# Attention's exponentials scaled where they lie, and modulation weights loaded by blocks of rows

## The chip, the cores and the metric

The kernel runs on one core of a Trainium2 chip. The core has five engines that run side by side, each with its own stream of instructions, taken in order: TensorE (PE in the profile; its weight loads are PEld), VectorE (DVE), ScalarE (ACT), GpSimd (POOL) and SyncE (SP, which here only issues transfers). They work on an on-chip memory of 128 partitions, SBUF, and on PSUM, into which TensorE writes. Semaphores tell one engine that another has finished. The metric is the device time of one execution in microseconds; the kernel's time is the median of several.

## The reference, cut to what matters

Two layers of a diffusion transformer over 256 context and 512 latent tokens, all in fp32. From a conditioning vector each layer gets six rows of 1024 numbers, shifts, scales and gates ("modulation"). Three mixers follow one input projection, of which one is attention and one a gated delta rule; then come the output projection, a gated layer norm and an MLP.

```python
mod_l = (jax.nn.silu(c) @ mod_w[i] + mod_b[i])[:, None, :]
mod_c = (jax.nn.silu(c_ctx) @ mod_w[i] + mod_b[i])[None, None, :]

def _attend(q, k, v):
    s = jnp.einsum('bqhgd,bkhd->bhgqk', q, k).astype(jnp.float32) * (HEAD_DIM ** -0.5)
    pr = jax.nn.softmax(s, axis=-1).astype(v.dtype)
    return jnp.einsum('bhgqk,bkhd->bqhgd', pr, v)
```

Attention has six query heads on two key heads of 64. A latent query sees all 768 keys, a context query the 256 context keys. The second layer needs only latent queries.

## The kernel before

**The order of the work.** The kernel is written as Python generators (scans, preparations, attention, modulation, projections), each of which issues a few instructions and yields. A planner, the class `Flow` (lines 40 to 195), keeps a planned time for each engine and tile from `cost` (line 74) and steps the generator whose planned time is lowest; tasks of the delta rule carry a bias that puts them ahead. So the order of instructions on each engine is set at build time by those estimates, and is then fixed. Every operation passes through one recorder, so all traced instructions have one line, L207; tiles tell them apart. PSUM is lent out in two kinds, four `mm` tiles of 128x512 and two `ax` tiles of 128x1024.

**The stage that the change touches.** Tokens come in tiles of 128: two of context, four latent. In each layer attention (`attention`, line 1041, and `att_out`, line 1095) runs side by side with the delta rule (`dn_make`, `dn_scan`, `dn_gate`, lines 1492 to 1595): roughly 320 to 590 us in layer 0, with all six tiles, and 1475 to 1690 us in layer 1, with the four latent ones. The scan is a chain of small matmuls (`S,rW`, `rr,rT`, `vn,rK`, `S,rQ`, `vn,rA` in the order's rows), and SP loads its `rT` tiles from scratch in HBM.

**Attention.** For each head: scores into an `ax` tile (`akh,qs` and `akl,qs`), the negated maximum `anm` on VectorE, the exponential `ape` on ScalarE with its sum, transposes of `ape` through an `mm` tile (`c_ident,ape`), copies into `apT` or `akT` on ScalarE, and for two heads together the product with the values (`apT,ava`, `akT,ava`). `ape` has two buffers. After six heads the reciprocals `ars` of the six sums are spread over partitions by twelve matmuls (`c_ident,ars`; six in the program), copied to `abc`, and multiplied into the output `ayb`, which is stored.

**Modulation.** `mod` (line 389) makes rows of the modulation: `cz` (the two conditioning vectors, 32 columns a block) times weights `modw`, K of 1024 in eight blocks of 128 rows, and n pieces of 512 columns that go to n groups of 32 partitions of one PSUM tile. Then the bias is added into `modb` and the rows are transposed (`c_ident,modb`). During layer 0's stage above, `mods` (line 859) runs `mod` for j=1 (n=4) and j=2 (n=2): 48 loads of 256 KB through four buffers. Stage 0 makes j=0 with `mod_in` (line 452), and later rows are made on VectorE in the MLP; the change touches neither.

**Layer 1's end.** `rest` (line 1645) starts the output projection. Its weights `wraw` (16 loads of 512 KB over both layers, rounded to `whi` by ScalarE) lie in memory that the delta rule's pool has used, so SP waits for the last gated output `zg`; broadcasts `lg`, `lb` and `g` stand in the same queue.

Of the kernel before, what the change touches and what calls it, by code (L numbers as in the profile page):

```python
# [8 lines left out]
F32 = mybir.dt.float32  # L9
F32R = mybir.dt.float32r  # L10
AF = mybir.ActivationFunctionType
ALU = mybir.AluOpType
# [4 lines left out]
P = 128  # L17
# [22 lines left out]
class Flow:  # L40
# [33 lines left out]
    def cost(self, eng, op, out, ins, kw):  # L74
        n = max([self.width(out)] + [self.width(a) for a in ins])
        if eng == "tensor":
            n, m = self.width(out), out.shape[0]
            if op == "transpose":
                return 0.87 * n
            if ins[-1].dtype == F32R:  # L80
                return max(35.0 + 0.56 * m, 0.42 * n)

            return (1.0 if m == 64 else 2.0) * max(35.0 + 0.62 * m, 0.83 * n)
        if eng == "vector":
            fast = op in ("tensor_copy", "tensor_scalar") and ins[0].tensor.name not in self.lent
            return 66.0 + n * (0.53 if fast else 1.04) + (60.0 if op == "scalar_tensor_tensor" else 0.0)
        if eng == "scalar":
            return 100.0 + 0.8 * n
        if eng == "gpsimd":
            return 160.0 + n * (170.0 if kw.get("op") == ALU.pow else 1.0 if op == "memset" else 2.1)  # L90
        return 4.0 * n * out.shape[0] / 340.0
# [133 lines left out]
def _half(f):  # L225
    return slice(64 * f, 64 * f + 64)


class Feed:
# [15 lines left out]
    def load(self):  # L245
        i = len(self.raws)
        src, n = self.srcs[i]
        t = self.pool.tile([P, WCOL], F32, tag="wraw", bufs=self.raw, name="wraw")[:, 0:n]
        self.k.nc.sync.dma_start(out=t, in_=src)
        self.raws.append(t)  # L250
# [34 lines left out]
class K:  # L285
# [103 lines left out]
    def mod(self, l, j, n, wt, bt, bufs):  # L389


        nc, d, flow = self.nc, self.d, self.flow
        mb = bt()
        nc.gpsimd.memset(mb, 0.0)
        for g in range(n):
            nc.sync.dma_start(
                out=mb[32 * g : 32 * g + 2, :], in_=d["mod_b"][l, j, g * 512 : g * 512 + 512].partition_broadcast(2)
            )
        ws = []

        def load(i):
            w = wt()
            nc.sync.dma_start(out=w, in_=d["mod_w"][l, j, i // n][:, (i % n) * 512 : (i % n) * 512 + 512])
            ws.append(w)

        for i in range(bufs):
            load(i)
        yield
        pm = yield from self.psum(512)
        for i in range(n * KD):  # L410
            k, g, w = i // n, i % n, ws.pop(0)
            yield flow.ready[w.tensor.name][0]
            nc.tensor.matmul(pm[32 * g : 32 * g + 32], self.cz[:, k, :], w, start=(k == 0), stop=(k == KD - 1))
            if i + bufs < n * KD:
                load(i + bufs)
                if i + bufs == n * KD - 1:
                    flow.signal(f"mw{l}{j}")
            yield
        ms = mb
        nc.vector.tensor_tensor(out=ms[0 : 32 * n], in0=pm[0 : 32 * n], in1=mb[0 : 32 * n], op=ALU.add)  # L420
        self.drop(pm)
        yield
        pt = yield from self.psum(512)
        for c in range(4):
            self.tr(pt[:, c * P : c * P + P], ms[:, c * P : c * P + P])
        yield
        ptv = pt.rearrange("p (c g s) -> p g c s", c=4, g=4)
        mt = self.modT[l]

        def take(name, g0, add):  # L430
            o = mt[name].rearrange("p (g c) s -> p g c s", g=2)
            nc.vector.tensor_scalar(out=o, in0=ptv[:, g0 : g0 + 2, :, 0:2], scalar1=float(add), scalar2=None, op0=ALU.add)

        def gate(w, g0):
            for s in range(2):
                for g in range(2):
                    r = 32 * (g0 + g) + s
                    nc.sync.dma_start(out=self.gates_d[l, w, s, g * 512 : g * 512 + 512].unsqueeze(0), in_=ms[r : r + 1, :])

        if j == 0:  # L440
            take("sh1", 0, 0)
            take("sc1", 2, 1)
        elif j == 1:
            gate(0, 0)
            take("sh2", 2, 0)
        else:
            take("sc2", 0, 1)
        self.drop(pt)
        self.flow.signal(f"mod{l}{j}")
        yield  # L450
# [223 lines left out]
class Kernel(K):  # L674
# [23 lines left out]
    def mix(self, l, xp, xh, xl, rest):  # L698
# [158 lines left out]
        AT.append(self.a_tiles(l, self.dn, 2))  # L857

        def mods():
            wt = lambda: self.dn.tile([P, 512], F32, tag="modw", bufs=4, name="modw")  # L860
            bt = lambda: self.dn.tile([P, 512], F32, tag="modb", bufs=1, name="modb")
            yield from self.mod(0, 1, 4, wt, bt, 4)
            yield from self.mod(0, 2, 2, wt, bt, 4)

        def makes(p):
            yield f"prep{l}{p}"
# [174 lines left out]
    def attention(self, l, at):  # L1041


        nc, ap_ = self.nc, self.a2
        qT, kT, va = at["qT"], at["kT"], at["va"]
        kh = ap_.tile([P, 2, TOK], F32R, name="akh")
        kl = ap_.tile([P, 2, TOK], F32R, name="akl")
        for c in (slice(0, CTX), slice(CTX, TOK)):
            for j in range(2):
                src = kT[_half(j), c]  # L1050
                for a in range(2):
                    nc.scalar.activation(out=kh[_half(a), j, c], in_=src, func=AF.Copy)
                for a in range(2):
                    nc.vector.tensor_tensor(out=kl[_half(a), j, c], in0=src, in1=kh[_half(j), j, c].bitcast(F32), op=ALU.subtract)
                yield
        late = None
        for t in self.tiles:
            n = CTX if t < 2 else TOK
            sl = slice(t * P, t * P + P)

            qs = ap_.tile([P, 3, 2, P], F32R, tag="qs", bufs=1, name="qs")
            for h2 in range(2):
                a, b = _half(h2), _half(1 - h2)
                nc.scalar.activation(out=qs[a, :, h2, :], in_=qT[a, :, sl], func=AF.Copy, scale=0.125)
                nc.vector.scalar_tensor_tensor(
                    out=qs[b, :, h2, :], in0=qT[a, :, sl], scalar=0.125, in1=qs[a, :, h2, :].bitcast(F32), op0=ALU.mult, op1=ALU.subtract
                )
            yield

            st = {"su": self.small([P, NH], "asu"), "pT": (ap_.tile([P, TOK], F32, tag="apT", bufs=1, name="apT"), kT)}  # L1070
            for m, h in enumerate(HEADS):
                q = qs[:, h // 2, h % 2, :]
                px = yield from self.psum(1024)
                ps = px[:, 0:n]
                for c in range(0, n, 512):
                    e = min(n, c + 512)
                    nc.tensor.matmul(ps[:, c:e], q, kh[:, h // 3, c:e], start=True, stop=False)
                    nc.tensor.matmul(ps[:, c:e], q, kl[:, h // 3, c:e], start=False, stop=True)
                yield
                if late:  # L1080
                    yield late
                nm = self.small([P, 1], "anm")
                nc.vector.tensor_reduce(out=nm, in_=ps, axis=AX.X, op=ALU.max, negate=True)
                yield
                i = NH * t + m
                if i - NH * self.tiles[0] > 1:
                    yield f"po{l}{i - 2}"
                pe = ap_.tile([P, TOK], F32, tag="ape", bufs=2, name="ape")
                nc.scalar.activation(out=pe[:, 0:n], in_=ps, func=AF.Exp, bias=nm[:, 0:1], accum_out=st["su"][:, h : h + 1])
                self.drop(ps)  # L1090
                yield
                late = self.att_out(l, t, m, n // P, pe, va, st)
        yield late

    def att_out(self, l, t, m, kts, pe, va, st):
# [29 lines left out]
        yield  # L1125
        if m < NH - 1:
            return

        rs = self.small([P, NH], "ars")
        nc.vector.reciprocal(rs, st["su"])  # L1130
        yield
        pb = yield from self.psum(384)
        for h in range(NH):
            nc.tensor.matmul(
                pb[_half(h % 2), h // 2 * P : h // 2 * P + P], rs[:, h : h + 1].broadcast_to([P, HD]), self.ident, start=True, stop=True
            )
        yield
        bc = ap_.tile([P, 384], F32, tag="abc", bufs=1, name="abc")
        nc.scalar.copy(bc, pb)
        self.drop(pb)  # L1140
        yield
        y = ap_.tile([P, 3, P], F32, tag="ayb", bufs=1, name="ayb")
        nc.vector.tensor_tensor(out=y, in0=pv, in1=bc.rearrange("p (a q) -> p a q", a=3), op=ALU.mult)
        self.drop(st["po"])
        yield from self.store(self.y_d[l, t, :, 2:5, :], y)

# [810 lines left out]
```

## Time and profile before

| | |
|---|---|
| median of 3 runs | 2119.76 us (2119.71 to 2125.24) |
| the profiled execution | 2125.93 us, span 2123.9 us |
| mean granted TensorE clock | 0.941 |
| TensorE busy | 1952.7 us, 92% |
| VectorE busy | 1339.7 us, 63% |
| ScalarE busy | 922.1 us, 43% |
| moved by DMA | 208.92 MB, mean 98 GB/s |

The span is the profiled execution from its first to its last instruction; the rest of its 2125.93 us lies around it. Busy shares are means over stages with different limits, so a term of a sum is read in the window where it lies. "Idle before, releaser" says what ended the wait of an engine. PEclk is the clock granted to TensorE as a share of 2.4 GHz; its other level, 1.2 GHz, shows as 0.50.

### The profile page before, as it was taken

Reading aid. Unit: us, or ns where it says so; the run is one execution under the profiler, and the core shown is the slowest. Engines: PE = TensorE matmul, PEld = TensorE weight load, DVE = VectorE, ACT = ScalarE, POOL = GpSimd, SP = SyncE. Lnnn points to the kernel's source line nnn. Section 1 sums busy time; section 2 is a strip of 40 time slices with the busy share of each in tenths; the row PEclk is TensorE's granted clock in tenths of the full one; section 3 lists DMA queues with packets and bytes.
Section 4 is the critical chain, followed back from the end, with each engine's and each line's share of the span. In section 5 each row is a group of like instructions: output and inputs, shape, how many; then the busy total and the mean of one; then the engine's idle time right before and its main releaser. Section 6 shows DMA issues by size and latency. Waiting matters only on the chain.

```text
span 2123.9 us, 31022 instructions
## 1 busy us (share of the span) xinstructions
PE 1952.7 (92%) x11960; PEld 1592.9 (75%) x11960; DVE 1339.7 (63%) x2499; ACT 922.1 (43%) x1881; POOL 195.3 (9%) x375
## 2 busy tenths in 40 slices
PE   6999779999998999999999989987898888999998
PEld 2788554667777888888888778776777668888886
DVE  5578787675477436362457776889785475544455
ACT  4444336467645422322232274543766535432331
POOL 1111211000012000000000111122100010000001
PEclk8999989989999999999999979977898999999999
DMA  7311014312335325241345233101101335332231
GB/s 278 101 45 51 26 49 142 106 56 58 126 107 185 119 74 166 80 139 45 135 160 184 88 136 96 52 34 33 28 20 28 119 127 186 119 100 80 85 114 60
DMA packets 98241, 208.92 MB, mean 98 GB/s; under 512 B 30851, under 2 KB 45059, under 8 KB 98093
## 3 DMA queue, kind: packets, MB, share of 16 engines
q1 hardware_dynamic: 86956, 189.24, 27.3%
q10 hardware_dynamic: 11136, 17.70, 2.3%
q8 instruction: 94, 1.54, 0.3%
q14 instruction: 55, 0.44, 0.1%
HBM read 184.38 MB, written 17.79 MB: 95 GB/s over the span
## 4 chain that ended last, share of the span: by engine, by line
PE 65%; DVE 16%; ACT 6%; issue 5%; POOL 4%; DMA 4%; SPq 0%; ACTq 0%; POOLq 0%; DVEq 0%
PE mm L207 41%; PE ax L207 24%; DVE cacc L207 2%; DVE wlo L207 2%; DVE tm L207 2%; DVE Xx L207 1%; POOL crn L207 1%; DVE M L207 1%; DVE A L207 1%; DMA wraw<-in_w_out 1%; POOL rs L207 1%; DVE axn L207 1%; DMA wraw<-in_w_up 1%; DVE st L207 1%; DMA modw<-in_mod_w 1%
## 5 line engine op out<-in xcount | busy, mean ns | idle before, releaser
L207 ACT ACTIVATE whi<-wraw 128x1024 fp32r<-128x1024 f32 (+2 forms) x188 | 195.1, 1050 | 449.7 <-PE ax L207 287.7
L207 DVE TENSOR_TENSOR wlo<-wraw,whi 128x1024 fp32r<-128x1024 f32 (+2 forms) x188 | 226.7, 1212 | 233.1 <-ACT whi L207 232.4
L207 PE MATMUL mm<-x2xh,whi 128*128 128x256 f32 (+1 forms) x832 | 287.0, 345 | 10.5 <-ACT whi L207 9.1
L207 PE MATMUL mm<-x2xl,whi 128*128 128x256 f32 (+1 forms) x832 | 286.3, 344 | 0.0
L207 PE MATMUL mm<-x2xh,wlo 128*128 128x256 f32 (+1 forms) x832 | 284.6, 342 | 0.9 <-DVE wlo L207 0.9
L207 PE MATMUL ax<-whi,hh 128*128 128x512 f32 x640 | 251.1, 392 | 0.1
L207 PE MATMUL ax<-wlo,hh 128*128 128x512 f32 x640 | 250.0, 391 | 0.1
L207 PE MATMUL ax<-whi,hl 128*128 128x512 f32 x640 | 249.9, 391 | 0.0
L207 PEld LDWEIGHTS mm<-x2xh,whi 128*128 128x128 f32 x832 | 159.2, 191 | 33.2 <-ACT whi L207 10.0
L207 DVE TENSOR_TENSOR acc<-acc,ax 128x1024 f32<-128x1024 f32 x68 | 82.9, 1219 | 148.2 <-PE ax L207 148.1
L207 PEld LDWEIGHTS mm<-x2xh,wlo 128*128 128x128 f32 x832 | 158.6, 191 | 20.2 <-DVE wlo L207 1.4
L207 PEld LDWEIGHTS mm<-x2xl,whi 128*128 128x128 f32 x832 | 159.0, 191 | 17.5
L207 PEld LDWEIGHTS ax<-whi,hh 128*128 128x128 f32 x640 | 120.2, 188 | 29.8 <-ACT hh L207 5.6
L207 PEld LDWEIGHTS ax<-wlo,hh 128*128 128x128 f32 x640 | 120.2, 188 | 27.4 <-issue 2.6
L207 PEld LDWEIGHTS ax<-whi,hl 128*128 128x128 f32 x640 | 120.1, 188 | 27.3 <-DVE hl L207 2.9
L207 DVE SCALAR_TENSOR_TENSOR acc<-modw,cz,acc 128x1024 f32<-128x1024 f32 x80 | 101.2, 1280 | 8.6 <-DMA acc<-in_mod_b 5.4
L207 ACT ACTIVATE rl<-mm 128x256 f32<-128x256 f32 (+1 forms) x104 | 50.5, 489 | 127.3 <-PE mm L207 127.3
L207 POOL TENSOR_SCALAR rs<-mv 128x1 f32<-128x1 f32 x52 | 33.0, 635 | 684.2 <-DVE mv L207 681.9
L207 PE MATMUL mm<-whi,yh 128*128 128x512 f32 x160 | 64.8, 415 | 10.7 <-ACT whi L207 9.3
L207 DVE TENSOR_REDUCE anm<-ax 128x1 f32<-128x768 f32 (+1 forms) x60 | 50.7, 847 | 36.2 <-PE ax L207 35.9
L207 DVE TENSOR_TENSOR hl<-rl,hh 128x768 fp32r<-128x768 f32 (+2 forms) x76 | 54.4, 716 | 28.0 <-ACT hh L207 28.0
L207 ACT ACTIVATE v<-mm,sh,sc 128x128 f32<-128x128 f32 x152 | 58.2, 463 | 29.3 <-PE mm L207 24.5
(256 smaller groups left out, 4276.7 us busy)
## 6 DMA issues: line engine op xcount, KB each, us to landing
wraw<-in_w_up SPq DMA_DIRECT2D x64, 512.0 KB
wraw<-in_w_down SPq DMA_DIRECT2D x64, 512.0 KB
modw<-in_mod_w SPq DMA_DIRECT2D x56, 512.0 KB
modw<-in_mod_w SPq DMA_DIRECT2D x80, 256.0 KB
wraw<-in_w_ch SPq DMA_DIRECT2D x22, 512.0 KB
wraw<-in_w_out SPq DMA_DIRECT2D x16, 512.0 KB
x_d<-xt ACTq DMA_DIRECT2D x16, 512.0 KB
xt<-x_d SPq DMA_DIRECT2D x14, 512.0 KB
```

The costliest lines, as they stand in the source:

```text
L207: return f(*args, **kw)
```

## The change

Three edits. First, `cost` prices a matmul of 32 rows by 512 columns at 0.6 ns a column, 307 ns, where it was 850; this shifts the planned times, and with them the order. Second, `mod` loads the n pieces of a block of rows in one transfer (1 MB for j=1, 512 KB for j=2; 16 loads for 48) and runs its n matmuls one after the other; in `mods` there is one buffer of 128x2048 in place of four of 128x512. Third, attention takes the reciprocal of each head's sum on VectorE and multiplies the exponentials by it in place, before they are transposed; the twelve matmuls, `abc` and the product go, and ScalarE copies the output from PSUM.

```diff
@@ cost
+            if m == 32 and n == 512:
+                return 0.6 * n
             return (1.0 if m == 64 else 2.0) * max(35.0 + 0.62 * m, 0.83 * n)
@@ mod
-        def load(i):
-            w = wt()
-            nc.sync.dma_start(out=w, in_=d["mod_w"][l, j, i // n][:, (i % n) * 512 : (i % n) * 512 + 512])
+        def load(k):
+            w = wt()[:, 0 : 512 * n]
+            nc.sync.dma_start(out=w, in_=d["mod_w"][l, j, k][:, 0 : 512 * n])
             ws.append(w)
...
-        for i in range(n * KD):
-            k, g, w = i // n, i % n, ws.pop(0)
+        for k in range(KD):
+            w = ws.pop(0)
             yield flow.ready[w.tensor.name][0]
-            nc.tensor.matmul(pm[32 * g : 32 * g + 32], self.cz[:, k, :], w, start=(k == 0), stop=(k == KD - 1))
-            if i + bufs < n * KD:
-                load(i + bufs)
-                if i + bufs == n * KD - 1:
-                    flow.signal(f"mw{l}{j}")
+            for g in range(n):
+                nc.tensor.matmul(
+                    pm[32 * g : 32 * g + 32], self.cz[:, k, :], w[:, 512 * g : 512 * g + 512], start=(k == 0), stop=(k == KD - 1)
+                )
+            if k + bufs < KD:
+                load(k + bufs)
             yield
@@ mods
-            wt = lambda: self.dn.tile([P, 512], F32, tag="modw", bufs=4, name="modw")
+            wt = lambda: self.dn.tile([P, 2048], F32, tag="modw", bufs=1, name="modw")
...
-            yield from self.mod(0, 1, 4, wt, bt, 4)
-            yield from self.mod(0, 2, 2, wt, bt, 4)
+            yield from self.mod(0, 1, 4, wt, bt, 1)
+            yield from self.mod(0, 2, 2, wt, bt, 1)
@@ attention
-                nc.scalar.activation(out=pe[:, 0:n], in_=ps, func=AF.Exp, bias=nm[:, 0:1], accum_out=st["su"][:, h : h + 1])
+                su = self.small([P, 1], "asu")
+                nc.scalar.activation(out=pe[:, 0:n], in_=ps, func=AF.Exp, bias=nm[:, 0:1], accum_out=su)
                 self.drop(ps)
                 yield
+                rs = self.small([P, 1], "ars")
+                nc.vector.reciprocal(rs, su)
+                nc.vector.tensor_scalar(out=pe[:, 0:n], in0=pe[:, 0:n], scalar1=rs[:, 0:1], scalar2=None, op0=ALU.mult)
+                yield
@@ att_out
-        rs = self.small([P, NH], "ars")
-        nc.vector.reciprocal(rs, st["su"])
...
-        bc = ap_.tile([P, 384], F32, tag="abc", bufs=1, name="abc")
-        nc.scalar.copy(bc, pb)
...
         y = ap_.tile([P, 3, P], F32, tag="ayb", bufs=1, name="ayb")
-        nc.vector.tensor_tensor(out=y, in0=pv, in1=bc.rearrange("p (a q) -> p a q", a=3), op=ALU.mult)
+        nc.scalar.copy(y, pv)
```

Since the planner sets the order, the change moves instructions. The rows that follow are of TensorE's order in layer 0's stage, in the second half of the modulation rows j=1; `modw,cz` are the modulation matmuls, the others steps of scans. First of before:

```order
1190 L207 MATMUL mm_67<-rr,rT_2721 128x128 x2
1191 L207 MATMUL mm_67<-vn,rK_2726 128x128 x2
1192 L207 MATMUL mm_69<-modw,cz 32x512
1193 L207 MATMUL mm_68<-S,rW_2742 128x128 x2
1194 L207 MATMUL mm_69<-modw,cz 32x512
1195 L207 MATMUL mm_68<-rr,rT_2747 128x128 x2
1196 L207 MATMUL mm_69<-modw,cz 32x512
1197 L207 MATMUL mm_68<-vn,rK_2752 128x128 x2
1198 L207 MATMUL mm_69<-modw,cz 32x512
1199 L207 MATMUL mm_68<-S,rQ_2757 128x128 x2
1200 L207 MATMUL mm_68<-vn,rA_2762 128x128 x2
```

The same place of the changed kernel (`kq` are key-query products of a later scan step, `c_ident,modb` the transposes that end j=1):

```order
1170 L210 MATMUL mm_66<-S,rQ_2757 128x128 x2
1171 L210 MATMUL ax_71<-akh,qs 128x256
1172 L210 MATMUL ax_71<-akl,qs 128x256
1173 L210 MATMUL mm_69<-modw,cz 32x512 x4
1174 L210 MATMUL ax_70<-kq 64x128 x8
1175 L210 MATMUL mm_69<-modw,cz 32x512 x20
1176 L210 MATMUL mm_69<-c_ident,modb 128x128 x4
1177 L210 MATMUL mm_69<-S,rW_2742 128x128 x2
1178 L210 MATMUL mm_69<-rr,rT_2747 128x128 x2
1179 L210 MATMUL mm_69<-vn,rK_2752 128x128 x2
```

Where single modulation matmuls stood between the steps of scans, 20 of them, the last five blocks of rows, now stand in one piece, ahead of the transposes and the next step `S,rW`.

SP's order at the same place, with the loads of `modw` and of `rT`. First of before:

```order
53 L207 DMA rT_2695<-TT_1019 64x2x64 x2
54 L207 DMA modw<-in_mod_w 128x512 x2
55 L207 DMA rT_2695<-TT_1019 64x2x64 x2
56 L207 DMA modw<-in_mod_w 128x512 x6
57 L207 DMA rT_2773<-TT_1024 64x2x64
58 L207 DMA modw<-in_mod_w 128x512
59 L207 DMA rT_2773<-TT_1024 64x2x64 x3
60 L207 DMA modw<-in_mod_w 128x512
```

and of the changed kernel:

```order
50 L210 DMA rT_2695<-TT_1019 64x2x64 x4
51 L210 DMA rT_2773<-TT_1024 64x2x64 x2
52 L210 DMA modw<-in_mod_w 128x2048
53 L210 DMA rT_2773<-TT_1024 64x2x64 x2
54 L210 DMA modw<-in_mod_w 128x2048 x3
55 L210 DMA modw<-in_mod_w 128x1024
56 L210 DMA gates_d<-modb 1x512 x4
57 L210 DMA rT_2747<-TT_1019 64x2x64 x2
58 L210 DMA rT_2721<-TT_1024 64x2x64
```

The last three loads of j=1 and the first of j=2 follow each other on SP; the loads of `rT` and the rows' stores to `gates_d` come behind them.

The last place is TensorE's order at the end of layer 1's stage; `whi,yh` is the first matmul of the output projection, `zg` the gated output of the delta rule. First of before:

```order
6479 L207 MATMUL mm_69<-akT,ava 64x128
6480 L207 MATMUL mm_69<-apT,ava 64x128
6481 L207 MATMUL mm_69<-akT,ava 64x128
6482 L207 MATMUL mm_69<-apT,ava 64x128
6483 L207 MATMUL mm_69<-akT,ava 64x128
6484 L207 MATMUL ax_70<-c_ident,zg 128x128 x4
6485 L207 MATMUL mm_67<-whi,yh 128x512
```

and of the changed kernel:

```order
6405 L210 MATMUL ax_71<-akh,qs 128x512
6406 L210 MATMUL ax_71<-akl,qs 128x512
6407 L210 MATMUL ax_71<-akh,qs 128x256
6408 L210 MATMUL ax_70<-c_ident,zg 128x128 x4
6409 L210 MATMUL ax_71<-akl,qs 128x256
6410 L210 MATMUL mm_69<-c_ident,ape 128x128 x4
6411 L210 MATMUL mm_66<-c_ident,ape 128x128 x2
6412 L210 MATMUL ax_70<-akh,qs 128x512
6413 L210 MATMUL ax_70<-akl,qs 128x512
6414 L210 MATMUL ax_70<-akh,qs 128x256
```

The transposes of `zg` stood behind attention's last product and just ahead of the projection; now they stand among the scores of the last heads. On SP the broadcasts `lg`, `lb` and `g`, which followed the first three loads of the projection's weights, now precede them.

## Rows read from the trace of the kernel before

**Rows 1.** The page: busy times (1) and the chain that ended last (4).

```profile
PE 1952.7 (92%) x11960; PEld 1592.9 (75%) x11960; DVE 1339.7 (63%) x2499; ACT 922.1 (43%) x1881; POOL 195.3 (9%) x375
...
PE 65%; DVE 16%; ACT 6%; issue 5%; POOL 4%; DMA 4%; SPq 0%; ACTq 0%; POOLq 0%; DVEq 0%
```

**Rows 2.** Windows: start:end, length, busy us (instructions) by engine, PEclk, DMA, GB/s.

```profile
320.00:590.00 270.00, 246.19 (x1960) 179.45 (x1958) 167.38 (x498) 167.20 (x512) 17.10 (x46) 0.94 0.31 95
...
1475.00:1690.00 215.00, 183.95 (x1715) 153.60 (x1716) 146.64 (x450) 142.07 (x417) 22.54 (x93) 0.88 0.14 37
...
1400.00:1500.00 100.00, 78.11 (x727) 64.53 (x726) 86.19 (x209) 50.63 (x107) 26.18 (x97) 0.76 0.12 37
...
1500.00:1600.00 100.00, 89.81 (x744) 75.40 (x746) 83.48 (x270) 65.00 (x196) 2.04 (x3) 0.97 0.09 20
```

**Rows 3.** Tile modw, 250 to 480 us: the matmuls, and TensorE's waits.

```profile
L207 PE MATMUL mm<-modw,cz x96: 592/617/1063, 318.9 to 433.3; 128*32 128x512 f32 x96
...
  DMA modw<-in_mod_w: 1.8, 4
```

**Rows 4.** Timeline, TensorE: start us, us, operation, xcount; then [idle before].

```profile
34.85 2.77 PE L207 MATMUL mm<-modw,cz 128*32 128x512 f32 x12
...
363.00 1.05 PE L207 MATMUL mm<-modw,cz 128*32 128x512 f32 x4
...
363.98 0.71 PE L207 MATMUL mm<-S,rQ 128*128 128x128 f32 x4
...
366.91 1.05 PE L207 MATMUL mm<-modw,cz 128*32 128x512 f32 x2
...
367.89 0.44 PE L207 MATMUL mm<-c_ident,gs 128*128 128x128 f32 x2
```

**Rows 5.** Timeline, SP's issue and ScalarE's start: two 512 KB loads landing.

```profile
1684.60 1.29 SPq L207 DMA_DIRECT2D wraw<-in_w_out  x3
...
1688.38 1.06 ACT L207 ACTIVATE whi<-wraw 128x1024 fp32r<-128x1024 f32 x1 [3.19 <-DMA wraw<-in_w_out]
...
1689.76 1.06 ACT L207 ACTIVATE whi<-wraw 128x1024 fp32r<-128x1024 f32 x1 [0.32 <-DMA wraw<-in_w_out]
```

**Rows 6.** Windows (columns as in rows 2) around that place.

```profile
1685.00:1690.00 5.00, 0.51 (x1) 0.50 (x2) 0.53 (x1) 1.49 (x3) 0.00 (x0) 0.50 0.89 288
...
1690.00:1695.00 5.00, 4.96 (x16) 3.47 (x15) 3.15 (x3) 1.87 (x2) 0.00 (x0) 0.72 1.03 391
```

**Rows 7.** Waits of TensorE, 320 to 590 us: total us, times, longest.

```profile
PE ax L207 <- DVE zg L207: 3.1, 2, 2.7
...
PE mm L207 <- ACT whi L207: 2.6, 1, 2.6
```

**Rows 8.** Groups by form: operation xcount | busy us, mean ns | idle before.

```profile
L207 PE MATMUL mm<-c_ident,ars 128*64 128x128 f32 x120 | 10.9, 280 | 0.0
...
L207 DVE RECIPROCAL ars<-asu 128x6 f32<-128x6 f32 x10 | 1.9, 190 | 3.1 <-ACT ape L207 3.0
...
L207 DVE TENSOR_TENSOR ayb<-mm,abc 128x384 f32<-128x384 f32 x10 | 5.5, 551 | 4.9 <-ACT abc L207 4.9
...
L207 ACT COPY abc<-mm 128x384 f32<-128x384 f32 x10 | 4.8, 483 | 8.3 <-PE mm L207 8.2
...
L207 DVE TENSOR_SCALAR be<-be 128x72 f32<-128x72 f32 x2 | 0.4, 204 | 0.0
...
L207 DVE TENSOR_TENSOR M<-M,be 128x768 f32<-128x768 f32 x12 | 11.0, 948 | 0.0
...
L207 DVE TENSOR_REDUCE anm<-ax 128x1 f32<-128x768 f32 x48 | 45.7, 954 | 30.3 <-PE ax L207 30.1
```

**Rows 9.** Timeline of TensorE at layer 1's end; waits of SP, 1600 to 1700.

```profile
1683.41 1.12 PE L207 MATMUL ax<-c_ident,zg 128*128 128x128 f32 x4 [3.03 <-DVE zg L207]
...
1689.49 0.79 PE L207 MATMUL mm<-whi,yh 128*128 128x512 f32 x1 [4.97 <-ACT whi L207]
...
SPq L207 <- DVE zg L207: 20.5, 1, 20.5
```

More of the change, by code (lines that the diff above doesn't have):

```diff
@@ L399, in mod @@
         ws = []
-        def load(i):
-            w = wt()
-            nc.sync.dma_start(out=w, in_=d["mod_w"][l, j, i // n][:, (i % n) * 512 : (i % n) * 512 + 512])
+        def load(k):
+            w = wt()[:, 0 : 512 * n]
+            nc.sync.dma_start(out=w, in_=d["mod_w"][l, j, k][:, 0 : 512 * n])
             ws.append(w)
-        for i in range(bufs):
-            load(i)
+        for k in range(bufs):
+            load(k)
         yield
         pm = yield from self.psum(512)
-        for i in range(n * KD):
-            k, g, w = i // n, i % n, ws.pop(0)
+        for k in range(KD):
+            w = ws.pop(0)
             yield flow.ready[w.tensor.name][0]
-            nc.tensor.matmul(pm[32 * g : 32 * g + 32], self.cz[:, k, :], w, start=(k == 0), stop=(k == KD - 1))
-            if i + bufs < n * KD:
-                load(i + bufs)
-                if i + bufs == n * KD - 1:
-                    flow.signal(f"mw{l}{j}")
+            for g in range(n):
[4 more added lines that the diff above has]
+                load(k + bufs)
             yield
@@ L1068, in attention @@
             yield
-            st = {"su": self.small([P, NH], "asu"), "pT": (ap_.tile([P, TOK], F32, tag="apT", bufs=1, name="apT"), kT)}
+            st = {"pT": (ap_.tile([P, TOK], F32, tag="apT", bufs=1, name="apT"), kT)}
             for m, h in enumerate(HEADS):
@@ L1127, in att_out @@
             return
-        rs = self.small([P, NH], "ars")
-        nc.vector.reciprocal(rs, st["su"])
[L1131 to L1137, printed above, removed]
-        bc = ap_.tile([P, 384], F32, tag="abc", bufs=1, name="abc")
-        nc.scalar.copy(bc, pb)
-        self.drop(pb)
-        yield
         y = ap_.tile([P, 3, P], F32, tag="ayb", bufs=1, name="ayb")
-        nc.vector.tensor_tensor(out=y, in0=pv, in1=bc.rearrange("p (a q) -> p a q", a=3), op=ALU.mult)
+        nc.scalar.copy(y, pv)
         self.drop(st["po"])
```

## The prediction, made before the changed kernel ran

> **What bounds the kernel now.** I read the page first. TensorE is busy for 92% of the span, VectorE for 63% and ScalarE for 43%, and the chain that ended last runs through TensorE for 65% [rows 1]. So work taken off TensorE is worth its own length, and a stretch in which TensorE can do nothing is lost, unless it shortens a later wait. Then I cut out the two stretches in which attention and the delta rule run, by windows: in layer 0 (320 to 590 us) TensorE works 246.2 of 270 us and VectorE 167.4; in layer 1 (1475 to 1690 us) 184.0 of 215 and 146.6 [rows 2]. In layer 0, then, TensorE idles for 24 us in all, and VectorE has some 100 us free; in layer 1, 31 and 68. Third, the tile view of the modulation weights: their 48 loads cost TensorE 1.8 us of waiting in four waits, so four small buffers hide the transfers almost wholly [rows 3]. That is the cover that the change takes away.
>
> **Modulation weights: TensorE's work.** A modulation matmul (two instructions) holds TensorE for 0.98 us: 366.91 to 367.89. Two of them on different groups of 32 columns take the same 0.98 us: 363.00 to 363.98 [rows 4]. The timeline has for the 32 matmuls of the first block of rows (j=1) 17 lone ones, five pairs, a slow first three (3.5 us) and two in a row on one column group (1.9): 22 x 0.98 + 5.4 = 27 us. For the 16 of j=2 it has seven pairs and two lone ones, 8.8 us. After the change a load feeds four (j=1) or two (j=2) matmuls that stand next to each other. Six matmuls in pairs took 2.77 us, 0.92 a pair [rows 4]; that four on four column groups also take one 0.98 is not in the trace. So j=1 takes between 8 x 0.98 = 8 us (four together) and 8 x 2 x 0.92 = 15 us (two pairs); j=2 takes 8. The gain is 13 to 20 us. I take 13, from the pairs, which the trace shows.
>
> **Modulation weights: the waits.** There is one buffer. Load k+1 may start only when the last matmul of block k has read it, and the next matmul waits for the landing. What that costs depends on what stands between two blocks in TensorE's order. TensorE's order (the first piece shown with the change) has it: after the third block eight small matmuls, and then 20 modulation matmuls without anything between, that is five blocks of 1 MB, one behind the other. TensorE takes its instructions in order, so nothing covers those loads. The price of one: 512 KB issued at 1684.60 let ScalarE begin at 1688.38, 3.8 us later, and the second 512 KB of the same burst 1.4 us after that [rows 5]; so 1 MB takes about 5.2 us. No load of 1 MB stands in this kernel, so I bound it by 3.8 (that 1 MB lands as 512 KB do) and 6.0 (2.4 us of start, and 1 MB at the 288 GB/s of that window [rows 6]). Five loads: 5 x 5.2 = 26, less 1 for the eight small matmuls: +25 (18 to 29). Between the first three blocks stand 17 to 19 rows of other work each: +2 (0 to 5). The eight loads of j=2 are 512 KB, 3.8 us each, with two to six short matmuls between them and the last two side by side; I put 0 to 2 us on six of them and 3.7 on the last: +7 (3 to 12). What waits behind this: on TensorE the transposes of the modulation rows and the next scan step; on SP the loads of rT, which follow the blocked weight loads in its order; on VectorE the sum of bias and matmul. None of it can come sooner, and all then comes together.
>
> A long idle also lowers the clock that TensorE is granted. Between 1685 and 1690 us it worked 0.51 us and the clock stood at 0.50, that is 1.2 GHz; in the next 5 us, busy throughout, the mean was still 0.72 [rows 6], so some 2.8 us of them ran at the lower level and gave up 1.4. One such recovery is 1.4; the serial blocks, whose matmuls run in between, and the stretch behind may see more. I take +3 (0 to 6). Against it, ScalarE and VectorE catch up while TensorE stands, so later waits shrink. The largest waits in the stretch add up to 3.1 and 2.6 us, both not near this place [rows 7]: I take -2 (-4 to 0).
>
> The Trainium skill speaks on both sides here. "DMA: Bandwidth & Descriptors", section Bandwidth, asks for batches of at least 1 MiB and gives 6.15 us for 1 MB; by that figure the five loads would be 31 us and the sum 5 higher (an estimate from that page). "Trainium Kernel Development and Optimization", Best Practices, asks for double buffers, so that DMA and compute overlap; the change keeps the first rule and breaks the second. The trace bears out the second: four buffers leave 1.8 us of waiting [rows 3].
>
> **Attention: what goes.** For each of ten tiles 12 instructions with the reciprocal sums, 10.9 us in all [rows 8]: six tiles in layer 0, -5 after their overlap with neighbours (-6.5 to -4); four in layer 1, of which the last stand in a stretch that waits anyway, -2. On VectorE one reciprocal (0.19) and one product (0.55) go per tile; on ScalarE a copy of 0.48 is replaced by another of the same size. The last tile of layer 0 loses a link between its matmuls and the store: -1.
>
> **Attention: what comes.** For each of 60 heads a reciprocal 128x1 (as 0.19) and a scaling of the exponentials in place stand between exponential and transposes. No tensor-by-scalar operation of this size is in the trace. The nearest by operation takes 0.20 us at 128x72, the nearest by size is a tensor-by-tensor product 128x768, 0.95 us [rows 8]. I take 0.95, for size decides. Layer 0 then gets 24 x 1.14 + 12 x 0.6 - 6 x 0.74 = 30 us more on VectorE, layer 1 24 x 1.14 - 4 x 0.74 = 24 us. Both fit in the free 100 and 68 us of [rows 2], so I charge only the delay: a head's chain (maximum 0.95, exponential, transposes) gets 1.2 to 1.3 us longer. Two score tiles and two exponential tiles are in flight, so most of that hides behind the other head's matmuls and the scans. Bounds: nothing, or 6 (layer 0) and 8 (layer 1), from some six heads each in which nothing else is left. I take +2 and +3. The Trainium skill ("VectorE: DVE Perf Modes", the perf-mode tier table) gives fp32 tensor-by-scalar work in SBUF twice the rate of tensor-by-tensor: 0.5 us as an estimate, by which the +3 would be +2 and the rival on VectorE less likely; no row here shows it.
>
> **The end of layer 1.** Now TensorE waits 3.03 us for the gated delta output (zg) and then 4.97 us for the first rounded tile of the output weights [rows 9], because those weights are loaded into memory that is free only when zg is done; SP waits 20.5 us for it [rows 9]. In the new order the transposes of zg stand two heads of attention earlier, so the loads and three 512 KB broadcasts run behind the attention. The 8 us can't all go, since attention's last chain then ends the stage: -6 (-9 to 0).
>
> **The sum.** Layer 0: 25 + 2 + 7 + 3 - 2 - 13 - 5 - 1 + 2 = +18. Layer 1: -6 - 2 + 3 = -5. Together +13. The profiled execution took 2125.93 us (span 2123.9), so 2139 in its frame; it lies 6 us above the median of 2119.76. Against the median: 2133 us, slower by 0.6%.
>
> **The rivals.**
> Faster: the wider loads pay. Each of the five waits costs 3.8 instead of 5.2, four matmuls run as one (-20 instead of -13), j=2 costs 3, the clock does not fall and layer 1 gives 9. 18 + 2 + 3 - 2 - 20 - 5 - 1 + 2 - 9 - 2 + 3 = -11, 2109 us. It decides at an exposed wait of about 3 us per block if the rest stays as in my sum. For it: 390 GB/s stands in a window of this trace [rows 6], which is 2.7 us for 1 MB. Against it: the first landing alone takes 3.8. It is also what the page's rule on batches would promise. Chance 0.22.
> No change: the five waits are there, but the other engines use them to run ahead. TensorE idles 24 us in layer 0's stretch; if 10 to 12 of them come back instead of 2, the sum is +3 to +5, 2124 us. Against it: waits in this stretch are many and short. Chance 0.15.
> Slower still: VectorE becomes the bound where scan and scaling meet. In layer 1 VectorE works 86.2 of 100 us from 1400 to 1500 and 83.5 from 1500 to 1600 [rows 2], so of the 24 us some 15 have no gap, and layer 0's last heads lose 6: 13 + 15 + 4 = +32, 2152 us. It decides once the scaling takes near 0.95 us and the heads fall in the full slices. Chance 0.13.
> My forecast, 2126 to 2150: chance 0.50.
>
> **How the numbers follow.** The range 2106 to 2156 holds the forecast and nearly all of the others; below lies part of the first rival, above the upper bounds of the loads with the third. A difference under 0.3% (6 us) can't be told from none. Faster: the first rival, 0.22. Same: the second and the near edge of the forecast, 0.17. Slower: the rest, 0.61.
>
> **What would show it.** In the changed kernel's tile view of the modulation weights, TensorE's waits for their DMA should be 30 to 40 us in some 13 waits, five of them near 5 us in a row, with VectorE idle there and the granted clock below 1. The modulation matmuls should hold TensorE 16 to 23 us instead of 36. The reciprocal matmuls are gone; the scaling should take 0.5 to 0.95 us. At the end of layer 1 the wait for the output weights should be under 2 us. If the five waits are below 3 us each, or work stands between them, the forecast is wrong on the low side; if VectorE is above 95% in layer 1's stretch, on the high side.

## The result and the profile after

The changed kernel takes 2152.64 us in the median (2151.01 to 2157.53), the kernel before, run beside it, 2121.44: ratio 1.0148, 95% interval 1.0125 to 1.0171. It is slower by 31 us, where I had forecast 13. The two profiled executions, 2125.93 and 2151.97 us, differ by 26.

The page of the changed kernel, busy times and the chain that ended last; [rows 1] are the same of before:

```profile
PE 1930.1 (90%) x11840; PEld 1582.0 (74%) x11840; DVE 1366.9 (64%) x2599; ACT 924.4 (43%) x1881; POOL 195.2 (9%) x375
...
PE 61%; DVE 18%; issue 7%; ACT 6%; DMA 4%; POOL 3%; SPq 0%; ACTq 0%; DVEq 0%; POOLq 0%
```

TensorE is busy 23 us less than before, VectorE 27 us more, and the span is 26 us longer: it is waiting that grew. To see where, I cut both traces at the same instructions: layer 0's stage from the first transpose `c_ident,gs` to the first matmul of the projection `whi,yh`, and layer 1's in the same way. Windows of the changed kernel (columns as in rows 2), layer 0 and layer 1:

```profile
319.90:625.40 305.50, 233.95 (x1887) 175.47 (x1887) 183.04 (x560) 168.46 (x515) 19.13 (x58) 0.86 0.28 86
...
1521.50:1723.20 201.70, 173.99 (x1574) 143.91 (x1570) 155.13 (x479) 141.89 (x413) 20.25 (x79) 0.92 0.19 52
```

and of the kernel before:

```profile
318.00:587.40 269.40, 245.37 (x1959) 178.44 (x1959) 166.71 (x500) 167.33 (x515) 18.88 (x57) 0.94 0.31 98
...
1477.90:1689.50 211.60, 180.74 (x1623) 150.47 (x1619) 143.30 (x440) 140.17 (x412) 20.05 (x79) 0.89 0.14 36
```

Layer 0's stage grew by 36.1 us, while TensorE's work in it fell by 11.4; its idle time went from 24.0 to 71.6 us. Layer 1's stage lost 9.9 us, and the projection behind it (first to last `whi,yh`) went from 58.2 to 50.0, another 8.2. What is left to the 26 us is 1.9 before layer 0's stage and 6.2 in the rest.

Where did layer 0 lose it? TensorE's timeline of the changed kernel at the modulation matmuls of j=1 (x8 is four matmuls; the idle time before and its cause stand in brackets; [rows 4] are single ones and pairs):

```profile
345.40 1.06 PE L210 MATMUL mm<-modw,cz 128*32 128x512 f32 x8
...
351.64 1.94 PE L210 MATMUL mm<-modw,cz 128*32 128x512 f32 x8 [4.57 <-DMA modw<-in_mod_w]
...
358.96 1.94 PE L210 MATMUL mm<-modw,cz 128*32 128x512 f32 x8 [5.38 <-DMA modw<-in_mod_w]
...
366.00 1.93 PE L210 MATMUL mm<-modw,cz 128*32 128x512 f32 x8 [5.11 <-DMA modw<-in_mod_w]
...
372.80 1.93 PE L210 MATMUL mm<-modw,cz 128*32 128x512 f32 x8 [4.87 <-DMA modw<-in_mod_w]
...
379.59 1.94 PE L210 MATMUL mm<-modw,cz 128*32 128x512 f32 x8 [4.86 <-DMA modw<-in_mod_w]
```

Five blocks, one behind the other, each after a wait of 4.6 to 5.4 us: 24.8 us. The full list of TensorE's waits in the stage begins with them (total, times, longest; [rows 7] are two of before):

```profile
PE mm L210 <- DMA modw<-in_mod_w: 32.2, 10, 5.4
...
PE mm L210 <- DVE gs L210: 6.4, 4, 4.6
...
PE mm L210 <- DVE ape L210: 4.4, 3, 2.2
...
PE ax L210 <- ACT ape L210: 4.2, 5, 1.8
...
PE mm L210 <- ACT apT L210: 3.4, 5, 1.1
```

And the windows of that place in the changed kernel, 10 us each:

```profile
350.00:360.00 10.00, 2.98 (x16) 0.40 (x16) 5.75 (x12) 2.22 (x2) 0.00 (x0) 0.53 0.56 169
...
360.00:370.00 10.00, 2.83 (x16) 0.20 (x8) 0.00 (x0) 0.00 (x0) 0.00 (x0) 0.50 0.42 123
...
370.00:380.00 10.00, 2.34 (x12) 0.40 (x16) 0.00 (x0) 0.00 (x0) 0.00 (x0) 0.50 0.52 192
...
380.00:390.00 10.00, 8.13 (x33) 5.53 (x26) 2.77 (x9) 0.56 (x2) 1.57 (x3) 0.50 0.20 60
```

and of the kernel before, for the 40 us together:

```profile
350.00:390.00 40.00, 37.11 (x217) 20.45 (x208) 23.27 (x76) 17.55 (x59) 0.00 (x0) 1.00 0.45 136
```

From 360 to 380 us VectorE and ScalarE did nothing at all, and TensorE's granted clock stood at 0.50 to 0.53, that is at or near 1.2 GHz, through the serial blocks and until 390. Before, TensorE was busy for 37.1 of these 40 us at the full clock; now it is busy for 16.3. The same four matmuls take 1.06 us at 345.40 and 1.93 us here.

### The profile page after: what moved, and what is told of

Read it like the earlier page. It is cut to its first block, busy times and chain, and to the rows that moved or that the text cites. A ratio compares the mean times of both kernels' runs of the same rounds, so it can differ in the third digit from the quotient of the medians.

```text
span 2150.0 us, 30808 instructions
## 1 busy us (share of the span) xinstructions
PE 1930.1 (90%) x11840; PEld 1582.0 (74%) x11840; DVE 1366.9 (64%) x2599; ACT 924.4 (43%) x1881; POOL 195.2 (9%) x375
## 4 chain that ended last, share of the span: by engine, by line
PE 61%; DVE 18%; issue 7%; ACT 6%; DMA 4%; POOL 3%; SPq 0%; ACTq 0%; DVEq 0%; POOLq 0%
PE mm L210 38%; PE ax L210 23%; DVE cacc L210 2%; DVE wlo L210 2%; DVE tm L210 2%; DVE Xx L210 2%; DMA modw<-in_mod_w 2%; POOL crn L210 1%; DVE M L210 1%; DMA wraw<-in_w_up 1%; DVE A L210 1%; DMA wraw<-in_w_out 1%; POOL rs L210 1%; DVE axn L210 1%; DVE st L210 1%
## 5 line engine op out<-in xcount | busy, mean ns | idle before, releaser
L210 PEld LDWEIGHTS ax<-whi,hl 128*128 128x128 f32 x640 | 120.1, 188 | 27.4 <-DVE hl L210 2.9
L210 PE MATMUL mm<-modw,cz 128*32 128x512 f32 x160 | 47.1, 772 | 39.7 <-DMA modw<-in_mod_w 39.7
L210 DVE SCALAR_TENSOR_TENSOR cacc<-cb,cw,cacc 128x772 f32<-128x772 f32 (+1 forms) x72 | 70.0, 973 | 0.7 <-ACT cacc L210 0.2
```

The source lines that it names most:

```text
L210: return f(*args, **kw)
```

## The experiments

All lengths are cut as above. "Wait" is TensorE's wait for `modw` in layer 0's stage, "busy" TensorE's busy time there, "projection" the one behind layer 1's stage; ratios are against runs of the kernel before on the same chip. These runs had a median of 2122.97 us beside e1_att to e4_plan, 2116.22 beside e4b_ready to e5_small and 2121.24 beside the last two, so kernels of different groups are compared by ratio and not by median.

| kernel | median us | ratio (95%) | wait | layer 0 | busy | layer 1 | projection |
|---|---|---|---|---|---|---|---|
| before | 2121.44 | | 0.3 | 269.4 | 245.4 | 211.6 | 58.2 |
| changed | 2152.64 | 1.0148 (1.0125 to 1.0171) | 32.2 | 305.5 | 234.0 | 201.7 | 50.0 |
| e1_att | 2110.15 | 0.995 (0.9931 to 0.9968) | 0.4 | 268.7 | 239.6 | 202.4 | 50.4 |
| e2_mod | 2157.26 | 1.0176 (1.0152 to 1.02) | 27.4 | 305.6 | 243.0 | 207.1 | 56.3 |
| e3_two | 2115.23 | 0.9968 (0.9952 to 0.9985) | 3.9 | 267.3 | 232.5 | 203.3 | 50.4 |
| e4_plan | 2163.79 | 1.0197 (1.0152 to 1.0241) | 1.7 | 267.5 | 228.8 | 202.5 | 50.4 |
| e4b_ready | 2102.91 | 0.9931 (0.9906 to 0.9956) | 0.7 | 256.1 | 225.6 | 202.5 | 52.0 |
| e7_cost | 2139.55 | 1.0096 (1.0059 to 1.0133) | 25.4 | 299.5 | 233.6 | 201.8 | 52.3 |
| e8_light | 2115.63 | 0.999 (0.997 to 1.0009) | 1.6 | 262.4 | 228.3 | 211.6 | 58.7 |
| e5_small | 2104.82 | 0.9941 (0.992 to 0.9963) | 1.7 | 267.9 | 237.9 | 198.6 | 50.1 |
| e9_ars | 2113.79 | 0.9971 (0.9951 to 0.9991) | 1.1 | 275.1 | 248.6 | 204.2 | 52.5 |
| e4b_again | 2103.65 | 0.9932 (0.9907 to 0.9957) | 0.9 | 255.6 | 225.0 | 202.2 | 52.1 |

My theory was that the exposed loads make the loss and attention's part the gain in layer 1. The rival was that the scaling on VectorE costs layer 0 half of its loss. The first two kernels split the change.

**Attention's part alone.** The diff is that of `attention` and `att_out` shown with the change; `cost`, `mod` and `mods` are those of before.

> Attention's part alone on the kernel before (modulation and its price in the plan as before). Theory A, that the loss is the exposed loads of the modulation weights and that attention's part gains in layer 1: TensorE waits under 4 us for modw, layer 0's stage (first c_ident,gs to first whi,yh) within 8 us of the 269 us of before, layer 1's stage and projection some 18 us shorter, 2103 to 2114 us. Rival B, that the reciprocals and scalings on VectorE cost layer 0 some 15 us or more: layer 0's stage 284 us or longer, 2120 us or more.

The window of layer 0's stage:

```profile
314.90:583.60 268.70, 239.61 (x1886) 170.31 (x1886) 184.19 (x559) 167.93 (x515) 19.68 (x58) 0.96 0.33 98
```

It is faster than the kernel before by 0.5%. VectorE has 17 us more work in layer 0's stage than before (184.2 for 166.7), and the stage is 0.7 us shorter. Rival B falls. Layer 1's stage and projection are 17.0 us shorter together, where 18 were expected.

**Modulation's part alone.** The diffs of `cost`, `mod` and `mods`; attention of before.

> Modulation's part alone (one load a block, one buffer, the new price in the plan), attention as before. Theory A: TensorE waits 28 to 36 us for modw, layer 0's stage 28 to 40 us longer than before, layer 1 as before: 2145 to 2165 us. Rival B: the waits are there but layer 0's stage is only 10 to 20 us longer, 2130 to 2142 us.

Its wait, among TensorE's waits in layer 0's stage:

```profile
PE mm L210 <- DMA modw<-in_mod_w: 27.4, 7, 5.2
```

The whole loss of layer 0 is here: its stage is as long as the changed kernel's (305.6 for 305.5), though the waits are a little under the 28 to 36 us expected. "Layer 1 as before" was a miss. The window of layer 1's stage:

```profile
1516.80:1723.90 207.10, 175.71 (x1622) 146.17 (x1618) 143.92 (x441) 140.09 (x412) 20.66 (x83) 0.91 0.15 38
```

Stage and projection are 6.4 us shorter than before, although attention is that of before and both waits of [rows 9] are still there (3.03 and 5.12 us). In the stage TensorE idles as long as before (31.4 for 30.9 us) and is busy 5.0 us less, at a mean clock of 0.91 for 0.89. So not all of what layer 1 gains belongs to attention.

**Two buffers of half the size.** A block of j=1 comes as two loads of 512 KB, and the second is under way while the first is used.

```diff
-            wt = lambda: self.dn.tile([P, 2048], F32, tag="modw", bufs=1, name="modw")
+            wt = lambda: self.dn.tile([P, 1024], F32, tag="modw", bufs=2, name="modw")
...
-            nc.sync.dma_start(out=w, in_=d["mod_w"][l, j, k][:, 0 : 512 * n])
+            nc.sync.dma_start(out=w, in_=d["mod_w"][l, j, k][:, 1024 * h : 1024 * h + 1024])
```

> The changed kernel with two buffers of 128x1024 in place of one of 128x2048, the same memory: loads of 512 KB, two matmuls each, the next load under way while a block is used. Theory A: waits for modw fall from 32 to under 8 us, layer 0's stage 270 to 282 us, 2105 to 2120 us. Rival B: the stage stays at 290 us or more, since attention holds it; 2128 us or more.

The wait falls from 32.2 to 3.9 us and the stage from 305.5 to 267.3, a little under the range of theory A, in the same memory.

**The same buffer, another order.** Is it the 1 MB load behind one buffer that costs, or that nothing stands between the blocks? The planner's `note` gives a load a start by SP's planned time and its source; it doesn't know that the tile has to be read out first. So in the plan all loads come early, and the blocks may follow each other. This kernel moves SP's planned time to the end of the last planned matmul ahead of each later load, in `mod` and also in `mod_dve`, which makes later modulation rows on VectorE and loads their weights on the same queue:

```diff
@@ mod
             if k + bufs < KD:
+                flow.free["sync"] = max(flow.free.get("sync", 0.0), flow.free["tensor"])
                 load(k + bufs)
...
@@ mod_dve
             if k + bufs < KD:
+                flow.free["sync"] = max(flow.free.get("sync", 0.0), flow.free["tensor"])
                 load(k + bufs)
```

> The changed kernel, one buffer of 128x2048 as it is, but the plan is told that a load starts only after the matmuls that free the buffer; the order then puts scans and scores between the blocks. Theory A (what costs is the order, the blocks without work between them, not the load of 1 MB): waits for modw under 10 us, none over 3, layer 0's stage 268 to 280 us, 2100 to 2118 us. Rival C (a 1 MB load behind one buffer costs by itself, in any order): waits for modw of 20 us or more, 2130 us or more.

TensorE's waits, the first line in layer 0's stage, the others from 660 to 1480 us:

```profile
PE mm L210 <- DMA modw<-in_mod_w: 1.7, 1, 1.7
...
PE mm L210 <- DVE acc L210: 18.7, 2, 14.8
...
PE mm L210 <- ACT xn L210: 13.4, 4, 5.1
...
PE ax L210 <- DVE y L210: 11.4, 1, 11.4
```

In the stage it does what theory A said: one buffer, loads of 1 MB, a wait of 1.7 us in all, 267.5 us. The order made the loss. Yet the kernel is the slowest of all, and the time stands elsewhere: from the end of layer 0's projection to layer 1's stage it takes 864.6 us, where before took 814.5. The last three lines are waits there, 43.5 us together (`acc` is the sum that `mod_dve` makes). The edit pushes SP's planned time for all that comes later, and ahead of each load of `mod_dve` once more: 20 of these loads were issued only between 1188.7 and 1229.2 us, where before had 4 left after 1150. Which of the two places cost it is not separated. So I told the plan of the landing alone, and in `mod` alone:

```diff
             nc.sync.dma_start(out=w, in_=d["mod_w"][l, j, k][:, 0 : 512 * n])
+            if k >= bufs:
+                t, e = flow.ready[w.tensor.name]
+                flow.ready[w.tensor.name] = (max(t, flow.free["tensor"] + 2200.0 + 4.0 * 512 * n * P / 340.0), e)
```

> The changed kernel, one buffer, with only the landing of each later block told to the plan (not earlier than the matmuls before it plus the load), and nothing else of the plan's clock for SP moved, as e4_plan did. Theory A: waits for modw under 8 us, layer 0's stage 264 to 274 us, and the 48 us that e4_plan lost between the stages gone: 2100 to 2118 us. Rival: the loss between the stages belongs to the order of the blocks; it stays, 2145 us or more.

Two blocks of j=1 in TensorE's timeline:

```profile
366.07 1.07 PE L210 MATMUL mm<-modw,cz 128*32 128x512 f32 x8
...
373.53 1.07 PE L210 MATMUL mm<-modw,cz 128*32 128x512 f32 x8
```

and the windows of the stage and of the 40 us in which the changed kernel stood:

```profile
317.70:573.80 256.10, 225.61 (x1887) 170.07 (x1887) 182.83 (x560) 167.11 (x515) 19.03 (x57) 0.94 0.34 103
...
350.00:390.00 40.00, 37.15 (x283) 27.03 (x283) 26.85 (x100) 22.78 (x81) 0.00 (x0) 1.00 0.46 138
```

No block of j=1 has a wait ahead of it, and TensorE is busy for 37 of the 40 us at the full clock. The stage is 8 us shorter than theory A's range, and the loss between the stages is gone (816.3 us). This kernel beats both: 0.9931 (0.9906 to 0.9956). It was run a second time:

> The kernel of e4b_ready once more, with more rounds and on the chip of e9_ars, for the interval: ratio to before 0.990 to 0.996, layer 0's stage 254 to 260 us, waits for modw under 2 us.

0.9932, and the stage at 255.6 us, confirm it.

**The price in the plan.** The changed kernel with the old price, 850 ns a modulation matmul.

> The changed kernel with the old price of a modulation matmul in the plan (850 ns for 307). Theory A (one buffer that the plan doesn't see makes the bare blocks): 16 matmuls still stand in one piece, waits for modw 24 to 36 us, 2140 to 2165 us. Rival D (the lower price packs the blocks together): waits under 12 us, 2125 us or less.

The wait is 25.4 us and the kernel 0.96% slower than before, so the new price isn't the cause, though some of the loss is its: 16 matmuls in one piece instead of 20, and three waits of 4.7 to 5.6 us in a row for five.

**Less TensorE work in layer 0's stage of the kernel before.** The theory had a hole: the modulation matmuls' saving didn't show. In e3_two and e4_plan TensorE is 13 to 17 us less busy than before, and the stage is only 2 us shorter. This kernel leaves out most columns of 42 of the 48 matmuls:

```diff
-            nc.tensor.matmul(pm[32 * g : 32 * g + 32], self.cz[:, k, :], w, start=(k == 0), stop=(k == KD - 1))
+            c = 512 if k == 0 else 64
+            nc.tensor.eng.matmul(pm[32 * g : 32 * g + 32, 0:c], self.cz[:, k, :], w[:, 0:c], start=(k == 0), stop=(k == KD - 1))
```

> The kernel before; of the 48 modulation matmuls of layer 0's stage the 42 after the first block of rows work on 64 columns in place of 512 (the rest of the sum is left out), loads and planned prices as before. It takes some 25 us of work off TensorE in that stage. Theory E (the work saved there is given back as waits, since scans and attention's tail set the stage): the stage gets 0 to 10 us shorter, 2112 to 2121 us. Rival F (TensorE bounds the stage, as predicted): 18 us or more shorter, 2103 us or less.

The window of layer 0's stage:

```profile
318.00:580.40 262.40, 228.29 (x1958) 183.16 (x1958) 166.33 (x500) 166.96 (x515) 19.04 (x57) 0.92 0.33 100
```

TensorE is 17.1 us less busy, not 25: the modulation matmuls hold it for 16.4 us instead of 38.0 (an instruction of 64 columns still takes 0.24 us, and a matmul is two), and the rest of its busy time is 4.5 us more, at a mean clock of 0.92 for 0.94. The stage is 7.0 us shorter, and the kernel's time the same within its interval. Six tenths of the work taken off came back as waits. That speaks for theory E, not for all of it.

**Less VectorE work in attention.** e1_att with the scaling on 32 columns only.

> Attention's part alone (as e1_att), with the scaling on 32 of the 768 or 256 columns (the others stay unscaled), planned price as before: VectorE loses some 20 us of work and each head's chain 0.4 us. Theory G (attention's chain sets the tail after the last scan): that tail falls from 61 to 55 us or less, 2098 to 2106 us against 2110 of e1_att. Rival H (the chain is hidden): within 3 us of e1_att.

From the last scan step's first matmul (`S,rW`) to the end of the stage, the tail, it is 61.5 us, in e1_att 61.2; layer 1's stage is 3.8 us shorter. The ratio, 0.9941, lies within the interval of e1_att's 0.995; the medians are of different groups. G falls for layer 0: the scaling's length doesn't set the tail there.

**Attention's twelve matmuls put back.** e1_att, with the matmuls issued into a PSUM tile that nobody reads.

> Attention's part alone (as e1_att), with the twelve matmuls a tile put back as work whose output nobody reads. Theory J (layer 1's gain comes from its end, where the output weights now land behind the last heads): layer 1's stage 202 to 206 us, and the projection behind it 50 to 52 us, as without them; 2108 to 2116 us. Rival K (the gain is the 4.4 us of matmuls that went): layer 1's stage and projection together 5 us or more longer than the 252.8 us of e1_att.

The windows of layer 0's and layer 1's stage:

```profile
316.70:591.80 275.10, 248.57 (x1958) 176.60 (x1958) 183.57 (x560) 169.03 (x515) 19.24 (x57) 0.95 0.32 96
...
1483.20:1687.40 204.20, 177.70 (x1622) 145.81 (x1618) 154.87 (x479) 142.45 (x413) 20.20 (x79) 0.92 0.18 49
```

Layer 1's stage and projection take 256.7 us together, 3.9 more than e1_att's 252.8, where before took 269.8. That is less than rival K's 5, and J's ranges hold for the stage (204.2) and just fail for the projection (52.5). The matmuls hold TensorE for 4.3 us in layer 1's stage, which is 1.8 longer. The projection has none of them; its idle time is as in e1_att (2.7 and 2.6 us) and its mean clock 0.90 for 0.97, so its 2.1 us are the clock's. So of the 17 us at most 4 are the matmuls, and 13 are something else, of which J's end is one part; e2_mod shows another. In layer 0 the matmuls hold TensorE for 6.5 us and the stage is 6.4 longer: there work put in did arrive. TensorE's busy time rose by more, 9.0, at a mean clock of 0.95 for 0.96.

## Why the prediction failed, step by step

**The waits** were sized right. Five serial loads: 25 predicted, 24.8 measured. All waits for modulation weights: 25 + 2 + 7 = 34 predicted, 24.8 + 0 + 7.4 = 32.2 measured. (The 1.8 us of [rows 3] are those of matmuls and weight loads together; matmuls alone waited 0.3 us, as in the table.) The price of 5.2 us for 1 MB, worked out from two landings [rows 5], stood between the measured 4.6 and 5.4. The sum by the figure of the Trainium skill ("DMA: Bandwidth & Descriptors", section Bandwidth), 31 us, was too high here. Its rule on batches and the rule on double buffers of "Trainium Kernel Development and Optimization", Best Practices, met head on, and neither decides alone: e3_two, with two buffers of 512 KB, waits 3.9 us, and e4b_ready, with one of 1 MB, waits 0.7, since its order puts other work between the loads.

**The clock** I put at 3. The changed kernel has 5.2 us more TensorE busy time in the stage than e4_plan (234.0 for 228.8), with the same matmuls in another order; mean granted clock 0.86 and 0.93. So 5 at least, of which the five serial blocks alone make 5 x 0.87 = 4.4. My estimate for all 16.3 us of work from 350 to 390 us, by the ratio of 1.06 to 1.93, is 7.3. The term was too small by 2 at least.

**The other engines' catching up**, -2, wasn't there, and the rival "no change", which hoped for 10 to 12, had nothing to stand on: the blocks are followed in TensorE's order by the scan's next step, and ScalarE and VectorE stood at 0.00. Nor did later waits shrink: without the waits for weights TensorE idles 39.4 us in the stage, where before it was 23.7.

**The saving on TensorE is the step that failed.** I wrote that work taken off TensorE is worth its own length, and put in -13 for the modulation matmuls and -5 for the reciprocal ones. The work did go: the modulation matmuls of the changed kernel hold TensorE for 26.0 us where it was 38.0, 12 for my 13, and e4_plan, which has all three edits without the stall, is 16.6 us less busy than before. The window of its stage in layer 0:

```profile
320.70:588.20 267.50, 228.78 (x1886) 172.13 (x1886) 183.16 (x559) 166.26 (x515) 18.93 (x57) 0.93 0.32 98
```

But that stage is 1.9 us shorter than before, at nearly the same clock, since idle time grew from 24.0 to 38.7. Take the waits (32.2) and the clock (5.2) from the changed kernel's 305.5, and 268.1 is left against 269.4: it gained 1 us, not 18 (3 with 7.3 for the clock). Layer 0 was +18 in my sum and is +36, and most of the gap of 18 is here. By parts, modulation alone (e2_mod) is +36.2 where 25 + 2 + 7 + 3 - 2 - 13 is +22, and attention alone (e1_att) is -0.7 where I had -4, so the gap lies mainly in modulation's part. In e2_mod TensorE is only 2.4 us less busy than before, at a mean clock of 0.85 for 0.94: there the clock took back much of what the matmuls had given. That chains of scan and attention stood close behind TensorE's 91% and took over is my reading; no run names the chain. How much arrives depends on the order: 7 of 17 us in e8_light, 2 of 17 in e4_plan, 13 of 20 in e4b_ready, 1 of 6 in e1_att, and in e9_ars 6.4 for 9.0 put in; these differences of busy time have the clock in them. What in an order decides this I can't say; it stays open.

**Attention's chain** in layer 0 (+2) can't be told from the saving beside it: e1_att is 0.7 us shorter than before where my terms -5 - 1 + 2 gave -4. With the matmuls put back (e9_ars) the stage is 5.7 us longer than before, so by that pair the matmuls were worth 6.4 and the rest of the edit, with its own order, cost 5.7. The length of the scaling isn't what costs: without most of it (e5_small) the stage is 0.8 us shorter. In layer 1, where I had +3, it is 3.8. The scaling took less than the 0.95 that I charged:

```profile
L210 DVE TENSOR_SCALAR ape<-ape,ars 128x768 f32<-128x768 f32 x48 | 29.6, 616 | 1.1
...
L210 DVE RECIPROCAL ars<-asu 128x1 f32<-128x1 f32 x60 | 9.4, 158 | 12.5 <-ACT ape L210 12.1
...
L210 DVE TENSOR_SCALAR ape<-ape,ars 128x256 f32<-128x256 f32 x12 | 4.1, 345 | 0.0
```

The rival with VectorE as the bound fell with e1_att and e5_small. That its time, 2152 us, is the one measured is chance.

**Layer 1** was -5 in my sum and is -18. The mechanism that I named was there, at the size that I gave it; more than half of the rest, some 8 us, is busy time that went with a higher clock, which I had left out. The timeline of the changed kernel at the end of layer 1's stage, with the loads' issue on SP, then the transposes of `zg` and the first matmul of the projection on TensorE:

```profile
1712.57 1.28 SPq L210 DMA_DIRECT2D wraw<-in_w_out  x3
...
1711.84 0.65 PE L210 MATMUL ax<-c_ident,zg 128*128 128x128 f32 x4 [1.45 <-DVE zg L210]
...
1723.24 0.73 PE L210 MATMUL mm<-whi,yh 128*128 128x512 f32 x2 [2.03 <-ACT whi L210]
```

and a window behind:

```profile
1725.00:1730.00 5.00, 5.00 (x23) 4.12 (x23) 3.08 (x4) 1.55 (x3) 0.00 (x0) 1.00 0.84 249
```

The waits of [rows 9] are 1.45 and 2.03 us for 3.03 and 4.97, because the loads are issued 10.7 us ahead of the first matmul, where before it was 4.9. That is 4.5 us, within my 0 to 9. What I left out is behind it. Before, the long wait had dropped the clock to 0.50, and the projection began at 0.72 [rows 6]; now the window 1725 to 1730 stands at 1.00, and the projection is 8.2 us shorter. The windows of the projection, before and changed:

```profile
1689.50:1747.70 58.20, 51.52 (x206) 39.76 (x207) 38.61 (x52) 21.24 (x35) 7.36 (x10) 0.91 0.45 158
...
1723.20:1773.20 50.00, 46.47 (x205) 36.66 (x206) 38.91 (x53) 21.02 (x35) 7.61 (x10) 1.00 0.41 134
```

TensorE does the same work in 5.1 us less, at 1.00 for 0.91, and waits 3.2 us less. Only part of the 5.1 is the recovery from the long wait: the clock of before falls a second time in the projection, to 0.85 and 0.81 from 1720 to 1740 us. The stage too ran at a higher clock (0.92 for 0.89) and is 6.7 us less busy; the reciprocal matmuls that went had held TensorE there for 4.0 (my term was 2, and put back in e9_ars they lengthen the stage by 1.8). I had priced a clock loss for layer 0 and none that could go in layer 1. Why layer 1 of before stands lower is open. e2_mod, with the end of before, already has 6.4 us of the 18. And part may be the execution that was profiled: that of before took 2125.93 us at 0.941, while 18 other runs of it (those beside e1_att) took 2113.94 to 2126.63 at 0.942 to 0.951.

So the sum was +13 for +31 by medians (+26 in the profiled executions): it was 18 too low in layer 0, 13 too high in layer 1, and 8 too low outside both, which I had at nothing. That these misses partly cancel is chance. The last 8 vary between runs of one kernel (the stretch from layer 0's projection to layer 1's stage took 816.3 and 821.8 us in two runs of the same program), and no cause is shown. The forecast's sign and its main mechanism, the exposed loads, held; its size didn't.

## What to carry to other kernels

Before pricing a deeper or larger transfer, look at what stands between two uses of its buffer in the order of the engine that waits: here five loads without work between them made TensorE wait 25 us, and the same loads with scans between them under 1. If a planner sets the order, it has to know when a buffer comes free, and telling it the landing times of the loads concerned went better here than moving the planned time of the whole queue ahead of every load. And work removed from an engine that is 91% busy isn't worth its length until a run has removed it alone: here between 2 of 17 and 13 of 20 us arrived.

## What the hardware showed that I hadn't expected

Four matmuls of 32 rows on four groups of columns take 1.06 us together, what one alone takes [rows 4]; I had counted on pairs. In the serial stretch TensorE worked 2.3 to 3.0 of every 10 us, and the granted clock stayed at 0.50 to 0.53, so each of these groups took 1.93 us. And the scaling in place takes 616 ns on 768 columns and 345 on 256: 0.53 ns a column, while the two tensor-by-tensor products of [rows 8] differ by (948 - 551) / 384 = 1.03 a column, though the shorter one reads PSUM. The Trainium skill's double rate ("VectorE: DVE Perf Modes", the perf-mode tier table) is there per column; the whole instruction is 0.65 of the tensor-by-tensor one of [rows 8] and not half, for a fixed 0.2 us (616 - 768 x 0.53) lies on top.
